# Striped expert channels, VectorE transposes and a split x in the expert stage of a two-layer streaming encoder on one core

## The chip, the core and the metric

The kernel runs on one core of one Trainium2 chip. The metric is the device time of one execution in microseconds (us). Before the change its median over 3 runs is 1421.37 us (1417.27 to 1430.04). All data is float32; "f32r" below is the rounded float32 type; a product of two f32r operands is one instruction of TensorE in the trace, a plain float32 product two.

## What is computed

Two layers over 256 tokens of width 1024. Each has a modulated norm, a convolution branch and an attention branch, an output product and a residual; then a feed-forward part. Layer 0 has a dense one. Layer 1 has eight experts, of which each token uses the two with the largest router logits:

```python
def moe_swiglu(h, w_router, b_router, w_gate, w_up, w_down):
    t = h.reshape(B * S, D)                                   # 256 x 1024
    logits = (t @ w_router) + b_router
    top_val, top_idx = lax.top_k(logits, TOP_K)               # TOP_K = 2
    top_w = jax.nn.softmax(top_val, axis=-1)
    combine = sum(one_hot(top_idx, 8) * top_w[..., None], axis=1)
    for e in range(8):                                        # w_gate, w_up: 1024 x 3584, w_down: 3584 x 1024
        out = out + combine[:, e:e + 1] * ((silu(t @ w_gate[e]) * (t @ w_up[e])) @ w_down[e])
```

The weights of the eight experts are 352 MB, three quarters of what the kernel reads.

## The kernel before, in words

Layer 0 and the attention half of layer 1 are untouched by the change, except for a small constant built at the start. All that follows is `moe`, the expert stage.

Tokens are dispatched. The experts are put into eight slots: slot 0 is expert 0, slots 1 to 7 hold the others by falling token count. `CAPS` gives each slot's room in groups of 32 tokens: (3, 4, 3, 3, 3, 2, 2, 2). Slot 1 with four groups is called wide, the rest narrow. `dispatch(e, pm)` makes the slot's tokens: `pick` compares token positions with a ramp and gives a 0/1 matrix `pm` (token x place), `gather` multiplies x by it on TensorE and applies the modulation, and a second product turns `pm` around into `pT`, which `combine` later uses to add the results back to their tokens. For a narrow slot `pT` comes from 8 products per group with the identity (L1076), for the wide one from two transposes (L1055).

An expert's 3584 hidden channels are walked in 7 pieces of 512. A unit is one slot and one piece: `gu_mm` (gate and up products, `silu`, product), `h_T` (transpose of the hidden piece on TensorE, copied back by ScalarE) and `dn_mm` (down product, accumulated in PSUM). Narrow slots use the four column strips of the TensorE array: in `streams` (L1089) a stationary block of 128 x 32 (one k block of one token group) is loaded into strip j, and 256 weight columns move past it; four strips work on four quarters of the columns side by side. The wide slot uses 128 x 128 stationary blocks and three f32r products of split operands (`mm3`, L254 to L256); ScalarE makes the high part of each weight tile (L140), VectorE the low part (L148).

TensorE's order is written out by hand. In each step of the unit loop: gate/up of unit n, then the down product of unit n-1, then the transposes of unit n, then, where due, a dispatch. `units` interleaves two lanes of slots, `LANES`; lane 1 starts three units (`STAGGER`) after lane 0. So with (0, 2, 1, 3) and (5, 4, 6, 7) the slot pairs that run together are 0/5, 2/5, 2/4, 1/4, 1/6, 3/6, 3/7.

Weights arrive in tiles of 1 MB (128 x 2048), all issued by SyncE (SP) in the order of use, six tiles per unit. The ring of buffers has 15 tiles where only narrow slots are near (9 `raw`, 3 `hi`, 3 `lo`), and 9 near the wide slot, whose high and low parts need the other six; a few spare buffers help at the start. A tile is loaded again when the last product that reads it is done. x stays in `x_sb`; the result gathers in a separate tile, `macc`.

Of the kernel before, what the change touches and what calls it, by code (L numbers as in the profile page):

```python
# [9 lines left out]
F32 = mybir.dt.float32  # L10
# [7 lines left out]
P = 128  # L18
D = 1024
# [18 lines left out]
LANES = (0, 2, 1, 3), (5, 4, 6, 7)  # L38
STAGGER = 3
NR = NE - 1  # L40
# [13 lines left out]
def kernel(ctx, tc, x, cvec, wada, bada, wga, wqkv, wout, wfgu, wfd, wfd2,  # L54
# [44 lines left out]
    for l in range(2):  # L99
        for n, w in (("ng1", 8), ("ng2", 8), ("cw", 4 * CW), ("cb", 4), ("lg", 4), ("lb", 4), ("qg", 1), ("kg", 1)):  # L100
# [14 lines left out]
                   allow_small_or_imprecise_dtypes=True)  # L115
    cs = const.tile([P, KT], F32, name="cs")
# [790 lines left out]
    def moe(acc, g_bc, mm, A, B, AW, bw):  # L907
        y = [None, None]
        oh = const.tile([P, 2, NT, NE], F32, name="oh")
# [106 lines left out]

        def gather(pm, n, put):

            for q in range(2):
                ps = bank("ps_g").rearrange("p (j s) -> p j s", j=4)  # L1020
                f = a2("xf", [P, 4, P])
                for j in range(4):
                    k = 4 * q + j
                    for t in range(NT):
                        nc.tensor.matmul(ps[:, j, 0:n], x_sb[:, t, k * P:(k + 1) * P], pm[:, 1, t, 0:n],  # L1025
                                         start=t == 0, stop=t == NT - 1)
                for j in range(4):
# [3 lines left out]
                put(slice(4 * q, 4 * q + 4), f[:, :, 0:n])  # L1031

        def dispatch(e, pm):


            g, n = CAPS[e], 32 * CAPS[e]
            src = gates if e else comb
            if wide(e):
                xg = a8("xg", [P, 2, KT, P], F32R)

                def put(js, f):
                    nc.scalar.activation(xg[:, 0, js, :], f, AF.Copy)
                    nc.vector.tensor_tensor(xg[:, 1, js, :], f, xg[:, 0, js, :].bitcast(F32), op=ALU.subtract)
            else:
                xg = a8("xn", [P, KT, n])

                def put(js, f):
                    nc.vector.tensor_copy(xg[:, js, :], f)

            gather(pm, n, put)  # L1050
            ps = bank("ps_ws")
            ws = sm.tile([P, 4], F32, tag="ws", name="ws")
            if wide(e):
                for tt in range(NT):
                    nc.tensor.transpose(ps[:, tt * P:(tt + 1) * P], pm[:, 0, tt, :], ident)  # L1055
                for tt in range(NT):
                    nc.tensor.matmul(ps[:, S:S + 1], pm[:, 0, tt, :], src[:, tt, e:e + 1], start=tt == 0,
                                     stop=tt == NT - 1)
                pT = a4("pmT", [P, S], F32R)
                nc.scalar.activation(pT, ps[:, 0:S], AF.Copy)  # L1060
                nc.vector.tensor_copy(ws[:, 0:1], ps[:, S:S + 1])
                return xg, pT, ws
            for t in range(g):
                for tt in range(NT):
                    for j in range(4):
                        nc.tensor.matmul(ps[32 * j:32 * j + 32, t:t + 1], pm[:, 0, tt, 32 * t:32 * t + 32],
                                         src[:, tt, e:e + 1], start=tt == 0, stop=tt == NT - 1)
            nc.vector.tensor_copy(ws[:, 0:g], ps[:, 0:g])
            pT = a4("pmT", [P, g, S], F32R)
            for b in range(0, g, 2):  # L1070
                ps = bank("ps_w").rearrange("p (t s) -> p t s", t=2)
                m = min(2, g - b)
                for t in range(m):
# [18 lines left out]
        def gu_mm(e, between):  # L1092


            g, xg = CAPS[e], disp[e][0]
# [10 lines left out]
            else:  # L1106
                pv = [p_.rearrange("p (t u s) -> p t u s", t=2, u=2) for p_ in ps]
# [19 lines left out]
        def h_T(hm, g, split=False):  # L1127
# [46 lines left out]
        def combine(e, ys, out_=None):  # L1174
# [12 lines left out]
            for b in range(0, 4, 2):  # L1187
# [10 lines left out]
                for i in range(2):  # L1198
                    sl = slice(256 * (b + i), 256 * (b + i) + 256)
                    nc.vector.tensor_tensor(macc[:, :, sl], (macc if e else x_sb)[:, :, sl], pss[i], op=ALU.add)  # L1200
# [7 lines left out]
        def rest(e):  # L1208

            pm = pick(lambda t: posm[:, t, 0:1])  # L1210
            xg = a8("xr", [P, KT, P])
            gather(pm, P, lambda js, f: nc.scalar.activation(xg[:, js, :], f, AF.Copy))
            ps = bank("ps_w")
            for t in range(NT):
                nc.tensor.transpose(ps[:, t * P:(t + 1) * P], pm[:, 0, t, :], ident)
            for t in range(NT):
                nc.tensor.matmul(ps[:, 2 * P:2 * P + 1], pm[:, 0, t, :], comb[:, t, 0:1], start=t == 0,
                                 stop=t == NT - 1)
# [67 lines left out]
        shares()  # L1286
        disp, accs = {0: dispatch(0, pm)}, {}
# [5 lines left out]
        with tc.manual_schedule():  # L1293
# [6 lines left out]
            for n, (e, c) in enumerate(units):  # L1300
# [15 lines left out]
                hm = gu_mm(e, between)  # L1316
                if n == 1:
# [11 lines left out]
                for pe, ys in early:  # L1329
                    if pe == 0:  # L1330
                        macc = a8("macc", [P, NT, D])
                    combine(pe, ys)
# [8 lines left out]
                pend = e, c, h_T(hm, CAPS[e], wide(e))  # L1341
# [170 lines left out]
```

## Time and profile before

| what | value |
|---|---|
| median of 3 runs | 1421.37 us (1417.27 to 1430.04) |
| the profiled execution: its time | 1421.24 us |
| its span (first to last instruction) | 1419.2 us |
| mean granted TensorE clock | 0.987 of 2.4 GHz |
| TensorE (PE) busy | 1349.9 us, 95% of the span |
| weight loads into the array (PEld) | 973.1 us, 69% |
| VectorE (DVE) / ScalarE (ACT) | 565.3 us, 40% / 398.4 us, 28% |
| read from HBM | 470.01 MB, 332 GB/s over the span |

The expert stage runs from 513 us, where the first slot is gathered, to the end. A row of a view of groups reads: line, engine, operation, output <- inputs, shapes, count | busy us, mean ns of one | idle time just before it and what ended most of it. Instructions of TensorE overlap, so count times mean is more than busy; the pace is read from the start of a run of instructions to the start of the next.

### The profile page before, as it was taken

Reading aid. Unit: us, or ns where it says so; the run is one execution under the profiler, and the core shown is the slowest. Engines: PE = TensorE matmul, PEld = TensorE weight load, DVE = VectorE, ACT = ScalarE, POOL = GpSimd, SP = SyncE. Lnnn points to the kernel's source line nnn. Section 1 sums busy time; section 2 is a strip of 40 time slices with the busy share of each in tenths; the row PEclk is TensorE's granted clock in tenths of the full one; section 3 lists DMA queues with packets and bytes.
Section 4 is the critical chain, followed back from the end, with each engine's and each line's share of the span. In section 5 each row is a group of like instructions: output and inputs, shape, how many; then the busy total and the mean of one; then the engine's idle time right before and its main releaser. Section 6 shows DMA issues by size and latency. Waiting matters only on the chain.

```text
span 1419.2 us, 38942 instructions
## 1 busy us (share of the span) xinstructions
PE 1349.9 (95%) x17604; PEld 973.1 (69%) x17604; DVE 565.3 (40%) x1025; ACT 398.4 (28%) x635; POOL 3.0 (0%) x17
## 2 busy tenths in 40 slices
PE   4998899999899999999999999999999999999886
PEld 4877699999697686657666656677667766665453
DVE  3597677777689651000100100354455430010011
ACT  3335444433456330101001001334333420100000
POOL 0000000000000000000000000000000000000000
PEclk9999999999999999999999999999999999999998
DMA  9963787878551579899999995989898999999995
GB/s 383 418 243 123 263 308 273 305 272 307 172 205 45 206 292 369 342 417 417 417 417 417 417 417 223 396 350 362 327 379 346 397 417 417 417 417 417 417 418 202
DMA packets 66379, 473.64 MB, mean 334 GB/s; under 512 B 7840, under 2 KB 7968, under 8 KB 9248
## 3 DMA queue, kind: packets, MB, share of 16 engines
q1 hardware_dynamic: 66208, 471.09, 83.3%
q8 instruction: 140, 2.29, 0.6%
q14 instruction: 31, 0.25, 0.0%
HBM read 470.01 MB, written 1.05 MB: 332 GB/s over the span
## 4 chain that ended last, share of the span: by engine, by line
PE 77%; DMA 13%; DVE 5%; ACT 3%; issue 1%; SPq 0%; DVEq 0%; ACTq 0%
PE ps_gu L1089 23%; PE ps_d L1089 13%; DMA raw<-in_wmgu 6%; DMA raw<-in_wmd 6%; PE ps_ga L256 4%; PE ps_ga L254 4%; PE ps_ga L255 4%; PE ps_g L1025 2%; PE ps_y L708 2%; PE ps_gu L256 2%; PE ps_gu L254 2%; PE ps_gu L255 2%; DVE cv L544 2%; PE ps_ada L308 1%; DVE lo L148 1%; PE ps_hT L1130 1%
## 5 line engine op out<-in xcount | busy, mean ns | idle before, releaser
L1089 PE MATMUL ps_gu<-raw,xn 128*32 128x256 f32 x8064 | 450.2, 380 | 4.1 <-DMA raw<-in_wmgu 3.9
L1089 PEld LDWEIGHTS ps_gu<-raw,xn 128*32 128x32 f32 x8064 | 269.1, 110 | 169.2 <-DMA raw<-in_wmgu 7.8
L148 DVE TENSOR_TENSOR lo<-raw,hi 128x2048 fp32r<-128x2048 f32 x99 | 225.5, 2289 | 84.7 <-ACT hi L140 82.0
L1123 DVE TENSOR_TENSOR mh<-ps_gu,sg 128x256 f32<-128x256 f32 (+1 forms) x91 | 32.7, 382 | 547.2 <-ACT sg L1120 547.2
L1089 PE MATMUL ps_d<-raw,hT 128*32 128x256 f32 x4032 | 232.3, 381 | 8.0 <-DMA raw<-in_wmd 7.5
L140 ACT ACTIVATE hi<-raw 128x2048 fp32r<-128x2048 f32 x99 | 188.3, 1912 | 107.2 <-PE ps_ga L256 43.0
L1089 PEld LDWEIGHTS ps_d<-raw,hT 128*32 128x32 f32 x4032 | 133.7, 110 | 96.6 <-DMA raw<-in_wmd 9.9
L1120 ACT ACTIVATE sg<-ps_gu 128x256 f32<-128x256 f32 (+1 forms) x91 | 32.0, 352 | 426.3 <-PE ps_gu L1089 380.7
L254 PE MATMUL ps_ga<-hThi,lo 128*128 128x256 f32 x480 | 137.5, 287 | 7.6 <-ACT hThi L446 7.6
L256 PE MATMUL ps_ga<-hTlo,hi 128*128 128x256 f32 x480 | 136.9, 285 | 0.8 <-DVE hTlo L451 0.8
L255 PE MATMUL ps_ga<-hThi,hi 128*128 128x256 f32 x480 | 136.3, 284 | 0.0
L254 PEld LDWEIGHTS ps_ga<-hThi,lo 128*128 128x128 f32 x480 | 92.9, 194 | 8.7 <-ACT hThi L446 8.4
L256 PEld LDWEIGHTS ps_ga<-hTlo,hi 128*128 128x128 f32 x480 | 92.4, 192 | 1.4 <-DVE hTlo L451 1.4
L255 PEld LDWEIGHTS ps_ga<-hThi,hi 128*128 128x128 f32 x480 | 92.4, 193 | 0.2
L544 DVE SCALAR_TENSOR_TENSOR cv<-zp,cols_sb,cv 128x256 f32<-128x256 f32 x206 | 85.4, 477 | 0.0
L1137 ACT ACTIVATE hT<-ps_hT 128x384 f32<-128x384 f32 (+1 forms) x49 | 21.8, 445 | 221.4 <-PE ps_hT L1130 221.4
L347 DVE SCALAR_TENSOR_TENSOR ada_acc<-raw,cs,ada_acc 128x512 f32<-128x512 f32 x63 | 47.2, 749 | 1.2
L256 PE MATMUL ps_gu<-lo,xg 128*128 128x512 f32 x112 | 44.3, 396 | 1.3 <-DVE lo L148 1.3
L254 PE MATMUL ps_gu<-hi,xg 128*128 128x512 f32 x112 | 44.8, 400 | 0.0
L255 PE MATMUL ps_gu<-hi,xg 128*128 128x512 f32 x112 | 44.3, 396 | 0.0
L308 PE MATMUL ps_ada<-raw,crep 128*32 128x128 f32 x960 | 34.4, 302 | 7.4 <-DMA raw<-in_wada 7.1
L308 PEld LDWEIGHTS ps_ada<-raw,crep 128*32 128x32 f32 x960 | 29.2, 121 | 11.2 <-issue 8.3
(263 smaller groups left out, 1310.1 us busy)
## 6 DMA issues: line engine op xcount, KB each, us to landing
raw<-in_wmgu SPq DMA_DIRECT2D x222, 1024.0 KB, 13.9
raw<-in_wmd SPq DMA_DIRECT2D x111, 1024.0 KB, 14.3
raw<-in_wada SPq DMA_DIRECT2D x48, 1024.0 KB, 6.2
raw<-in_wfgu SPq DMA_DIRECT2D x22, 1024.0 KB, 6.0
raw<-in_wqkv SPq DMA_DIRECT2D x12, 1024.0 KB, 6.6
raw<-in_wfd SPq DMA_DIRECT2D x11, 1024.0 KB, 6.5
raw<-in_wga SPq DMA_DIRECT2D x8, 1024.0 KB, 10.6
raw<-in_wout SPq DMA_DIRECT2D x8, 1024.0 KB, 7.7
```

The costliest lines, as they stand in the source:

```text
L140: nc.scalar.activation(hi[:, i * w:(i + 1) * w], r, AF.Copy)
L148: nc.vector.tensor_tensor(lo[:, w], r, hi[:, w].bitcast(F32), op=ALU.subtract)
L254: nc.tensor.matmul(o_, a[1], b[0], start=first, stop=False)
L255: nc.tensor.matmul(o_, a[0], b[0], start=False, stop=False)
L256: nc.tensor.matmul(o_, a[0], b[1], start=False, stop=last)
L308: nc.tensor.matmul(ps[32 * g:32 * g + 32, 0:P], crep[:, j, :], w(j)[:, g * P:(g + 1) * P], start=j == 0, stop=j == KT - 1)
L347: nc.vector.scalar_tensor_tensor(accs[ch], ws[ch](j), cs[:, j:j + 1], accs[ch], op0=ALU.mult, op1=ALU.add)
L544: nc.vector.scalar_tensor_tensor(cv[:, a, :], zp[:, a, i:i + S], cw[:, a, i:i + 1], cv[:, a, :], op0=ALU.mult, op1=ALU.add)
L708: nc.tensor.matmul(acc[t][hf], yf[:, k, t * P:(t + 1) * P], w(k // 2, 2 * (k % 2) + hf), start=k == 0, stop=False)
L1089: nc.tensor.matmul(ps[t // 2][32 * j:32 * j + 32, t % 2], x(t), w(j), start=first and t % 2 == 0, stop=last, skip_group_check=True)
L1120: nc.scalar.activation(sg[:, 2 * b:2 * b + m, :], v[:, 0:m, 0, :], AF.Silu)
L1123: nc.vector.tensor_tensor(hm[:, 2 * b:2 * b + m, :], v[:, 0:m, 1, :], sg[:, 2 * b:2 * b + m, :], op=ALU.mult)
```

## The change

1. `gu_mm` of a narrow slot. A weight tile pair m (256 gate and 256 up columns) is now multiplied by itself: for each k block one stationary block per strip and 128 moving columns, taken as 4 runs of 32 columns with a step of 128. Each strip thus holds, for every token, hidden channels striped so that a 32 x 32 block transpose gives the layout that the down product wants.
2. The hidden piece is turned by one VectorE `transpose` (32 x 32 blocks), `h_T` of a narrow slot does nothing, and TensorE's transposes and ScalarE's copy of them go. The wide slot keeps them.
3. x times its norm factor is split once, after unit 2, into f32r high and low parts (`split_x`); every `gather` but slot 0's multiplies both by the f32r `pm`.
4. `pT`: `row` spreads the positions of the 256 tokens over all partitions by two products with the identity, and VectorE compares them with the constant `spot`.
5. `macc` is `x_sb` itself; its old place holds other tiles (`home` for the gathered tokens of six slots).
6. The lanes become (0, 1, 2, 3) and (5, 6, 4, 7). Pairs: 0/5, 1/5, 1/6, 2/6, 2/4, 3/4, 3/7. The two halves of a gate/up tile pair are also loaded in the new order of use.

```diff
-LANES = (0, 2, 1, 3), (5, 4, 6, 7)
+LANES = (0, 1, 2, 3), (5, 6, 4, 7)
...
-        plan += [(of_slot(wmgu, e, *p), 4096 if wide(e) else 0) for p in (parts if wide(e) else zip(*parts))]
+        plan += [(of_slot(wmgu, e, *p), 4096 if wide(e) else 0) for p in parts]
...
-            pm = a2("pm", [P, 2, NT, P])
+            pm = a2("pm", [P, NT, P], F32R)
             for t in range(NT):
-                nc.vector.tensor_scalar(pm[:, 1, t, 0:n], iota_f[:, 0:n], col(t), y[t], op0=ALU.is_equal,
-                                        op1=ALU.mult)
-            for t in range(NT):
-                nc.vector.tensor_scalar(pm[:, 0, t, 0:n], iota_f[:, 0:n], col(t), None, op0=ALU.is_equal)
+                nc.vector.tensor_scalar(pm[:, t, 0:n], iota_f[:, 0:n], col(t), None, op0=ALU.is_equal)
...
+        def split_x():
+            hi = a8("xh", [P, NT, D], F32R)
+            lo = a8("xl", [P, NT, D], F32R)
+            for t in range(NT):
+                nc.scalar.activation(hi[:, t], x_sb[:, t], AF.Copy, scale=y[t])
+            for t in range(NT):
+                nc.vector.scalar_tensor_tensor(lo[:, t], x_sb[:, t], y[t], hi[:, t].bitcast(F32), op0=ALU.mult,
+                                               op1=ALU.subtract)
...
+                ops = [(v, pm[:, t, 0:n]) for t in range(NT) for v in parts[0][t]]
...
-                    for t in range(NT):
-                        nc.tensor.matmul(ps[:, j, 0:n], x_sb[:, t, k * P:(k + 1) * P], pm[:, 1, t, 0:n],
-                                         start=t == 0, stop=t == NT - 1)
+                    for i, (v, m) in enumerate(ops):
+                        nc.tensor.matmul(ps[:, j, 0:n], v[:, k * P:(k + 1) * P], m, start=i == 0,
+                                         stop=i == len(ops) - 1)
...
+        def row(col):
+            ps = bank("ps_w")
+            for t in range(NT):
+                nc.tensor.matmul(ps[:, t * P:(t + 1) * P], col(t).to_broadcast([P, P]), ident, start=True, stop=True)
+            return ps[:, 0:S]
...
-                        for j in range(4):
-                            nc.tensor.matmul(ps[32 * j:32 * j + 32, t, tt * P:(tt + 1) * P],
-                                             pm[:, 0, tt, 32 * (b + t):32 * (b + t) + 32], ident, start=True, stop=True)
-                nc.scalar.activation(pT[:, b:b + m, :], ps[:, 0:m, :], AF.Copy)
+                for t in range(g):
+                    nc.vector.tensor_scalar(pT[:, t, :], r, spot[:, 4 + t:5 + t], None, op0=ALU.is_equal)
...
-                for h in range(2):
+                pv = [p_.rearrange("p (t m a s) -> p t m a s", t=2, m=2, a=4) for p_ in ps]
+                for m in range(2):
                     w = whole(3)
-                    for i in range(4):
-                        k = 4 * h + i
-                        wk_ = [w(a, i).rearrange("p (u j s) -> p u j s", u=2, j=2) for a in range(2)]
-                        streams(pv, g, lambda t: xg[:, k, 32 * t:32 * t + 32], lambda j: wk_[j // 2][:, :, j % 2],
-                                k == 0, k == KT - 1)
+                    for k in range(KT):
+                        wk_ = w(k // 4, k % 4).rearrange("p (a j s) -> p j a s", a=4, j=4)
+                        streams([v[:, :, m] for v in pv], g, lambda t: xg[:, k, 32 * t:32 * t + 32],
+                                lambda j: wk_[:, j], m == 0 and k == 0, k == KT - 1)
...
+                hT = a2("hT", [P, g, P])
+                nc.vector.transpose(hT.rearrange("p t s -> p (t s)"), hm.rearrange("p t s -> p (t s)"))
+                return hT
...
-        def h_T(hm, g, split=False):
+        def h_T(hm, g, split=False, narrow=False):
+            if narrow:
+                return hm
...
                 hm = gu_mm(e, between)
+                if n == STAGGER - 1:
+                    parts.append(split_x())
```

How the instructions move is shown at three places. First TensorE before, at the end of slot 5's third unit, where slot 2 is dispatched: `ps_gu` is gate/up, `ps_d` the down product, `ps_hT` the transposes, `ps_g`, `ps_ws` and `ps_w` the dispatch.

```order
L1089 MATMUL ps_d_6035<-raw,hT 32x256 x32
L1130 MATMUL ps_hT<-ident,mh 128x128 x3
L1025 MATMUL ps_g<-pm,x_sb 128x96 x16
L1066 MATMUL ps_ws<-rt,pm 32x1 x24
L1076 MATMUL ps_w<-ident,pm 32x128 x24
L1089 MATMUL ps_gu_6458<-raw,xn 32x256 x64
L1089 MATMUL ps_d_5319<-raw,hT 32x256 x8
```

There the transposes follow the down product, then the dispatch, then the next unit.

TensorE after the change, the dispatch of slot 5 after unit 2 and the gate/up of the next unit (lines are those of the changed kernel):

```order
L1048 MATMUL ps_g<-pm,xh 128x64
L1048 MATMUL ps_g<-pm,xl 128x64
L1093 MATMUL ps_ws<-rt,pm 32x1 x16
L1060 MATMUL ps_w<-ident,rt 128x128 x2
L1114 MATMUL ps_gu_5886<-raw,xn 32x128 x8
L1114 MATMUL ps_gu_5887<-raw,xn 32x128 x4
```

The transposes between the down product and the next unit are gone, `ps_w` is 2 products in place of 24 (16 for a slot of two groups), the gather alternates the two parts of x, and a gate/up product has 128 moving columns, not 256.

TensorE after the change where the wide slot begins: slot 0's last unit, slot 5's unit, then slot 1.

```order
L1114 MATMUL ps_d_6553<-raw,hT 32x256 x32
L1114 MATMUL ps_gu_7534<-raw,xn 32x128 x128
L1114 MATMUL ps_d_5494<-raw,hT 32x256 x8
L1114 MATMUL ps_d_5495<-raw,hT 32x256 x4
L261 MATMUL ps_gu_7745<-hi,xg 128x512
L262 MATMUL ps_gu_7745<-hi,xg 128x512
L263 MATMUL ps_gu_7745<-lo,xg 128x512
```

A two-group unit has 128 gate/up products where it had 64, and the wide slot now follows slot 0; before, slot 2 stood there.

VectorE after the change, around unit 2: `mh` is the hidden piece, `xl` the low part of x, `xn` the gathered tokens.

```order
L1151 TENSOR_TENSOR mh<-ps_gu_5547,sg 128x256
L1151 TENSOR_TENSOR mh<-ps_gu_5548,sg 128x128
L1154 STREAM_TRANSPOSE hT<-mh 128x384
L1029 SCALAR_TENSOR_TENSOR xl<-x_sb,ny,xh 128x1024 x2
L1080 COPY xn<-xf 128x256 x2
L1095 COPY ws<-ps_ws 128x2
L1103 TENSOR_SCALAR pmT<-ps_w,spot 128x256 x2
```

The block transpose stands right behind the product that it turns, the split of x behind that, and the comparisons that make `pT` come last, where ScalarE copied a product before.

## Rows read from the trace of the kernel before

**Rows 1.** Busy time of each engine, five stretches of the expert stage.
```profile
core 0: us, PE busy (x) PEld busy (x) DVE busy (x) ACT busy (x) POOL busy (x), PEclk, DMA share, GB/s
519.00:860.00 341.00, 339.10 (x6097) 219.83 (x6097) 34.02 (x108) 38.07 (x97) 0.00 (x0) 1.00 0.99 404
860.00:920.00 60.00, 58.66 (x926) 37.11 (x926) 14.67 (x18) 15.81 (x25) 0.00 (x0) 1.00 0.74 290
920.00:1150.00 230.00, 228.54 (x2515) 163.59 (x2517) 111.31 (x97) 93.48 (x96) 0.00 (x0) 0.99 0.91 365
1150.00:1285.00 135.00, 135.00 (x2393) 82.86 (x2385) 14.03 (x33) 13.53 (x34) 0.00 (x0) 1.00 1.01 417
1285.00:1400.00 115.00, 103.44 (x1736) 58.18 (x1732) 8.54 (x18) 7.38 (x18) 0.00 (x0) 0.99 0.99 408
```

**Rows 2.** Costliest groups of the page: narrow products, and layer modulation in the 128-column form.
```profile
L1089 PE MATMUL ps_gu<-raw,xn 128*32 128x256 f32 x8064 | 450.2, 380 | 4.1 <-DMA raw<-in_wmgu 3.9
L1089 PE MATMUL ps_d<-raw,hT 128*32 128x256 f32 x4032 | 232.3, 381 | 8.0 <-DMA raw<-in_wmd 7.5
L308 PE MATMUL ps_ada<-raw,crep 128*32 128x128 f32 x960 | 34.4, 302 | 7.4 <-DMA raw<-in_wada 7.1
```

**Rows 3.** What SP's DMA queue waited for, 480 to 1420 us: total, times, longest.
```profile
SPq L131 <- PE ps_gu L1089: 248.4, 62, 9.6
SPq L131 <- PE ps_d L1089: 144.9, 34, 10.8
```

**Rows 4.** Chain of work in order of time (start, us, what): pairs 0/5 and 2/4.
```profile
660.32 10.50 PE ps_gu L1089 x192
...
674.27 0.48 PE ps_hT L1130 x3
...
686.98 0.37 PE ps_hT L1130 x2
687.35 10.50 PE ps_gu L1089 x192
...
809.18 10.50 PE ps_gu L1089 x192
...
841.50 10.50 PE ps_gu L1089 x192
```

**Rows 5.** The same chain: pairs 1/4 and 1/6, from one narrow down product to the next.
```profile
925.76 5.32 PE ps_d L1089 x96
...
959.50 5.32 PE ps_d L1089 x96
...
1069.91 3.59 PE ps_d L1089 x64
...
1098.36 3.59 PE ps_d L1089 x64
```

**Rows 6.** Timeline of PE: a burst of 128-column products, and one gate/up run of 256 columns.
```profile
504.68 1.96 PE L308 MATMUL ps_ada<-raw,crep 128*32 128x128 f32 x64
...
600.85 10.57 PE L1089 MATMUL ps_gu<-raw,xn 128*32 128x256 f32 x192
```

**Rows 7.** The chain again: dispatches of a two-group and a three-group slot.
```profile
571.39 0.92 PE ps_w L1076 x32
...
642.37 3.55 PE ps_g L1025 x32
...
646.41 1.36 PE ps_w L1076 x48
```

**Rows 8.** The chain at the first unit's end, and one f32r product of 512 columns.
```profile
529.70 0.39 ACT sg L1120
...
530.12 0.44 DVE mh L1123
...
1056.63 0.23 PE ps_d L255
```

**Rows 9.** Groups by form, 440 to 1420 us: transposes, and a VectorE copy.
```profile
L1130 PE MATMUL ps_hT<-ident,mh 128*128 128x128 f32 x154 | 28.7, 290 | 0.5 <-DVE mh L1123 0.5
...
L1048 DVE COPY xn<-xf 128x384 f32<-128x384 f32 x8 | 2.9, 360 | 23.1 <-ACT xf L1029 23.1
```

More of the change, by code (lines that the diff above doesn't have):

```diff
@@ L37 @@
 CAPS = (3, 4, 3, 3, 3, 2, 2, 2)
-LANES = (0, 2, 1, 3), (5, 4, 6, 7)
+LANES = (0, 1, 2, 3), (5, 6, 4, 7)
 STAGGER = 3
+HOME = (0, None, 0, None, 768, 768, 1536, 1536)
 NR = NE - 1
@@ L115 @@
                    allow_small_or_imprecise_dtypes=True)
+    spot = const.tile([P, 8], F32, name="spot")
+    nc.gpsimd.iota(spot[:, 0:4], pattern=[[32, 4]], base=1, channel_multiplier=1, allow_small_or_imprecise_dtypes=True)
+    for v in range(4):
+        nc.vector.tensor_scalar(spot[32 * v:32 * v + 32, 4:8], spot[32 * v:32 * v + 32, 0:4], -32.0 * v, None,
+                                op0=ALU.add)
     cs = const.tile([P, KT], F32, name="cs")
@@ L908, in moe @@
         y = [None, None]
+        macc, parts = x_sb, []
         oh = const.tile([P, 2, NT, NE], F32, name="oh")
@@ L1015, in slot_pick @@
             return pick(lambda t: src[:, t, e:e + 1], 32 * CAPS[e])
-        def gather(pm, n, put):
+        def split_x():
[6 more added lines that the diff above has]
+                                               op1=ALU.subtract)
+            return [(hi[:, t], lo[:, t]) for t in range(NT)]
+        def gather(pm, n, put):
+            if not parts:
+                sm_ = a2("pmy", [P, NT, P])
+                for t in range(NT):
+                    nc.vector.tensor_scalar(sm_[:, t, 0:n], pm[:, t, 0:n].bitcast(F32), y[t], None, op0=ALU.mult)
+                ops = [(x_sb[:, t], sm_[:, t, 0:n]) for t in range(NT)]
+            else:
+                ops = [(v, pm[:, t, 0:n]) for t in range(NT) for v in parts[0][t]]
             for q in range(2):
@@ L1031, in gather @@
                 put(slice(4 * q, 4 * q + 4), f[:, :, 0:n])
+        def row(col):
+            ps = bank("ps_w")
+            for t in range(NT):
+                nc.tensor.matmul(ps[:, t * P:(t + 1) * P], col(t).to_broadcast([P, P]), ident, start=True, stop=True)
+            return ps[:, 0:S]
         def dispatch(e, pm):
             g, n = CAPS[e], 32 * CAPS[e]
-            src = gates if e else comb
+            src, at = (gates, places) if e else (comb, posm)
+            pf = pm.bitcast(F32)
             if wide(e):
@@ L1044, in dispatch @@
             else:
-                xg = a8("xn", [P, KT, n])
+                xg = a8("xn", [P, G]) if HOME[e] is None else home[:, HOME[e]:HOME[e] + KT * n]
+                xg = xg[:, 0:KT * n].rearrange("p (k n) -> p k n", k=KT)
                 def put(js, f):
@@ L1054, in dispatch @@
                 for tt in range(NT):
[L1055 to L1061, printed above, removed]
@@ L1062, in dispatch @@
-                return xg, pT, ws
-            for t in range(g):
-                for tt in range(NT):
-                    for j in range(4):
[L1066 to L1073, printed above, removed]
+                    nc.tensor.matmul(ps[:, 0:1], pf[:, tt, :], src[:, tt, e:e + 1], start=tt == 0, stop=tt == NT - 1)
@@ L1079, in dispatch @@
+            r = row(lambda t: at[:, t, e:e + 1])
+            if wide(e):
+                pT = a4("pmT", [P, S], F32R)
+                nc.vector.tensor_scalar(pT, r, spot[:, 0:1], None, op0=ALU.is_equal)
+            else:
+                pT = a4("pmT", [P, g, S], F32R)
+                for t in range(g):
+                    nc.vector.tensor_scalar(pT[:, t, :], r, spot[:, 4 + t:5 + t], None, op0=ALU.is_equal)
             return xg, pT, ws
@@ L1199, in combine @@
                     sl = slice(256 * (b + i), 256 * (b + i) + 256)
-                    nc.vector.tensor_tensor(macc[:, :, sl], (macc if e else x_sb)[:, :, sl], pss[i], op=ALU.add)
+                    nc.vector.tensor_tensor(macc[:, :, sl], macc[:, :, sl], pss[i], op=ALU.add)
                 if out_:
@@ L1210, in rest @@
             pm = pick(lambda t: posm[:, t, 0:1])
+            pf = pm.bitcast(F32)
             xg = a8("xr", [P, KT, P])
@@ L1214, in rest @@
             for t in range(NT):
-                nc.tensor.transpose(ps[:, t * P:(t + 1) * P], pm[:, 0, t, :], ident)
+                nc.tensor.transpose(ps[:, t * P:(t + 1) * P], pf[:, t, :], ident)
             for t in range(NT):
-                nc.tensor.matmul(ps[:, 2 * P:2 * P + 1], pm[:, 0, t, :], comb[:, t, 0:1], start=t == 0,
+                nc.tensor.matmul(ps[:, 2 * P:2 * P + 1], pf[:, t, :], comb[:, t, 0:1], start=t == 0,
                                  stop=t == NT - 1)
@@ L1286, in moe @@
         shares()
+        home = a8("xn", [P, G])
         disp, accs = {0: dispatch(0, pm)}, {}
@@ L1340, in moe @@
                     ahead(2)
-                pend = e, c, h_T(hm, CAPS[e], wide(e))
+                pend = e, c, h_T(hm, CAPS[e], wide(e), not wide(e))
                 if nxt is not None:
```

21 lines of the change are left out of this document (18 added, 3 removed).

## The prediction

> **What bounds the kernel now.** First I read the busy time by stretches of the expert stage [rows 1]. From 519 to 1285 us TensorE is busy in 761 of 766 us, the granted clock at 0.99 to 1.00: it sets the pace there. From 1285 to 1400 us it is busy in 103.4 of 115, and the DMA share is 0.99: there the weights set the pace and TensorE waits 11.6 us, in the down and gate/up products, for `in_wmd` (7.5 us) and `in_wmgu` (3.9 us) [rows 2]. So the stage has two limits close together. A weight tile of 1.049 MB at 417 GB/s takes 2.51 us, six of them 15.1 us, a pair of units 30.2 us. TensorE, read from one gate/up to the same place a pair later, takes 27.0 us for the pair 0/5 and 32.3 for 2/4 [rows 4], 33.7 for 1/4 and 28.4 for 1/6 [rows 5]. Summed over the stretches, TensorE works 865 us and the tiles moved (342 MB) need 821 us. The DMA stood idle for some 58 us before 1150 us (rates of 404, 290 and 365 against 417 GB/s [rows 1]) because SP waited for TensorE to release buffers, 248 us behind gate/up and 145 us behind the down products [rows 3], and it lacked that time at the end, where light pairs (27.0 us of TensorE against 30.2 of DMA) emptied the ring.
>
> So a microsecond taken from TensorE before 1285 us counts fully: it also lets SP go on sooner. At the end it counts only if the ring no longer runs dry.
>
> **Part by part.** The sum is made against the profiled execution, 1421.24 us (span 1419.2 and 2.0 around it), which is the median of the runs shown within 0.2 us.
>
> *Transposes of narrow slots.* They stand on TensorE between the down product and the next gate/up: 0.48 us for three groups and 0.37 for two [rows 4]. Slots 0, 2, 3, 4 have 28 units of three groups, slots 5, 6, 7 have 21 of two: 28 x 0.48 + 21 x 0.37 = 21.2 us, the 126 of the 154 transposes that are not the wide slot's [rows 9]. In the first unit there is no down product between, so TensorE also waits 0.39 + 0.44 us for ScalarE and VectorE [rows 8]; that 0.8 us goes too, since the next gate/up now follows at once. Sum: -22.0 us.
>
> *The VectorE transpose in their place.* The trace has none. Its nearest row is the copy of 128x384 at 0.36 us [rows 9]; from below it is bounded by nothing, from above I take four such copies, 1.4 us. It is hidden in either case: its result is wanted after a whole further gate/up, over 7 us for two groups (128 instructions at 53 ns), and silu, product and transpose need 0.39 + 0.44 + 1.4 us after the end of their own. I take 0. If VectorE fell so far behind in the wide stretch (busy 111 of 230 us [rows 1]) that this cover were gone, at most 1.4 us would stand in a unit. The Trainium skill, "VectorE: DVE Perf Modes", section "The three transpose paths", gives 311 ns for 128x128 bf16 in 32x32 blocks on VectorE, which would make an estimated 0.9 us here; no row shows it, and it would be hidden as well.
>
> *Gate/up in 128 columns.* 8064 instructions of 256 columns become 16,128 of 128. The pace of 256 is (10.57 - 0.38) / 191 = 53.4 ns, the run of 192 less its last instruction [rows 6, 2]. For 128 columns with 128x32 blocks there are bursts: 64 instructions in 1.96 us, less 0.30 for the last, give 26.4 ns [rows 6, 2]; 48 against 32 instructions of `ps_w` differ by 0.44 us, 27.5 ns each [rows 7]. So 430.6 us become 425.8 to 443.5, that is -5 to +13; I take the middle, 26.95 ns, +4 us. The columns now come in runs of 32. Before, gate/up read two runs of 128 and the down product one of 256, and their durations are 380 and 381 ns [rows 2], so one jump costs nothing; three jumps have no row. The upper bound is the mean of the whole 128-column group, 34.4 us / 960 = 35.8 ns [rows 2], which would be +147 us; it holds starts and tails of short bursts, so I take the bursts themselves. It is the first rival below.
>
> *Turning `pm` around.* `ps_w` cost 1.36 us for three groups and 0.92 for two [rows 7]; now it is 2 products with 128x128 blocks, 4 instructions. At the gather's pace of 3.55 / 32 = 0.11 us [rows 7] that is 0.44. Four slots save 0.92, three save 0.48, the wide one trades 2 instructions for 4 (+0.2): -4.9 us. The comparisons on VectorE are wanted only when the slot is finished, seven units later: 0.
>
> *Gather from the split x.* Before: 16 float32 products of two instructions each; now 32 f32r products of one. 32 instructions with a 128x128 block and 64 to 128 columns before and after, and 3.55 us for 96 columns is 0.11 us each, more than 96 columns at the pace of [rows 6] need, so the block's load sets it. I take 0. Bounds for seven slots: at 26.4 ns each -19 us; at 0.23 us, what an f32r product of 512 columns takes [rows 8], +27 us. The split itself (two ScalarE and two VectorE instructions of 1024 columns, some 1 us each by the copy's 0.36 for 384) comes after unit 2's gate/up, beside a down product of 5.3 us [rows 5], and ends some 4 us into it: hidden, and at most 4 us, once, if not. Slot 0's gather now waits for one more pair of VectorE instructions: +0.4 us.
>
> *x in place of `macc`, `home`, the constant at the start.* Nothing of these is on TensorE; the store at the end is the same. 0.
>
> *The order of the lanes.* Before, after the last heavy pair came 4 of 1/6, 3 of 3/6, 4 of 3/7 and 3 units of slot 7 alone: against the DMA -1.8, -3.2, -3.2 each and some -4 for a unit alone (192 instructions at 53.4 ns and 0.37 us against 15.1), -41 us in all, against one or two dispatches of some 5 us, four combines, and a ring of 9 tiles (22.6 us) at the end of the wide slot. It ran dry at 1285 us. Now 2/4 and 3/4 come late: 32.3 less two transposes is 31.4, +1.2 each, so in those seven pairs the ring of 15 tiles (38 us) fills; after them come only 4 of 3/7 and 3 units alone, some -29 us, with one dispatch and three or four combines against it. The light pairs 0/5 and 1/5, 1/6 stand at the start, where the ring is full and five dispatches help. So the 11.6 us at the end go: -11.6. What is late next is the DMA itself: 821 us of tiles against 865 - 23 = 842 us of TensorE, 21 us of margin.
>
> Sum: -22.0 + 4 - 4.9 + 0.4 - 11.6 = -34.1 us: **1387.1 us**, 2.4% faster.
>
> **Rivals.** *The pace of 128 columns does not hold (slower).* Place: gate/up of all narrow units. The rows at 27 ns are bursts of 48 and 64; now runs of 256 and 384 follow each other, with twice the weight loads and moving runs of 32 columns. For: PEld is already busy 0.64 of the stretch from 519 us [rows 1], and the group mean is 35.8 ns. Against: the bursts show no slowing. Above 26.95 + 34.1 us / 16,128 = 29.1 ns the change loses. Half way between 27.5 and 35.8, at 31.6 ns, it costs 75 us: 1462 us. The Trainium skill's "TensorEngine Tiling (Array Packing)", section "Instruction Overhead", speaks against the change in the same place: some 60 cycles of overhead for each product. By that rule, 25 ns for 8064 more instructions shared by four strips, the estimate is 50 us and a time of 1437 us. The trace so far disagrees: 26.4 against 53.4 ns leaves no room for it.
>
> *The ring still runs dry at the end.* If the DMA, not TensorE, ends the stage, what TensorE gains after 1285 us turns into waiting. Its gains before that, some 36 of 49 narrow units, are 0.73 x 22.5 = 16 us, and SP follows them: about 1404 us. For it: the margin of 21 us is less than the 58 us for which the DMA stood, and the wide slot still has only 9 tiles. Against it: the pairs above.
>
> *The f32r gather is slow below 256 columns.* No row has one. At 0.23 us an instruction, +27 us: 1414 us. Against: 64 to 128 columns should not take what 512 take.
>
> *Nothing changes because the weights bound everything.* Excluded but for 3%: the tiles need 821 us, TensorE 865.
>
> **Chances.** Forecast 0.66, dry ring 0.12, slow gather 0.08, pace 0.11, others 0.03. The range goes from 1368 (gate/up at its low end, -9, and half of the gather's low bound, -10) to 1408 (past the dry ring, without the slow gather at its full price and the pace); about 0.18 lies outside. A measurement can tell about 1% from no change, 14 us: below 1407 lie the forecast, the dry ring and most of a milder slow gather, 0.84; within 1% 0.06; slower 0.10.
>
> **What would show it.** Right: no transposes of narrow slots on TensorE, gate/up of three groups in 10.3 to 10.6 us for 384 instructions, `ps_g` at 3.5 us, `ps_w` at 0.44, hardly any wait for `in_wmd` and `in_wmgu` in the last 115 us, a DMA share under 1 there. Wrong: gate/up runs over 11.2 us (29.1 ns), an idle TensorE ahead of `ps_d` put down to the VectorE transpose, waits for weights at the end, or gathers over 5 us.

## The result: a tenth slower

The changed kernel takes 1567.12 us (median of 4 runs, 1558.43 to 1569.90), the kernel before 1420.53 us in the same comparison: a ratio of 1.1015, 95% interval 1.0955 to 1.1075, or +146 us. The forecast was 1387.1 us. The profiled execution took 1565.86 us, with a span of 1564.2 us.

The page of the changed kernel, its two narrow products (columns as for [rows 2]):

```profile
L1114 PE MATMUL ps_gu<-raw,xn 128*32 128x128 f32 x16128 | 492.6, 280 | 110.9 <-issue 108.8
L1114 PE MATMUL ps_d<-raw,hT 128*32 128x256 f32 x4032 | 242.8, 387 | 14.4 <-issue 12.2
```

Where gate/up waited 4.1 us in all, and for weights [rows 2], it now stands idle 110.9 us, and 108.8 of that is put down to "issue": nothing that the profile shows was missing, no operand, no buffer, no other engine. The busy time is 42 us higher as well. Stretches of the expert stage (columns as for [rows 1]):

```profile
519.00:860.00 341.00, 301.03 (x6495) 256.56 (x6496) 101.83 (x153) 76.93 (x101) 0.00 (x0) 0.97 0.85 333
...
1000.00:1290.00 290.00, 243.02 (x6834) 215.07 (x6827) 29.47 (x71) 14.45 (x44) 0.00 (x0) 0.98 0.85 326
1290.00:1560.00 270.00, 230.86 (x6186) 205.74 (x6185) 31.16 (x68) 12.22 (x34) 0.00 (x0) 0.94 0.80 306
```

In [rows 1] either TensorE or the DMA was full in every stretch. Here TensorE is busy 0.84 to 0.88 of the time, the DMA share is 0.80 to 0.85: neither sets the pace. The timeline shows what the idle time looks like (start, length, run of like instructions, in brackets the idle time ahead of it):

```profile
635.10 3.70 PE L1114 MATMUL ps_gu<-raw,xn 128*32 128x128 f32 x128 [2.50 <-issue]
...
649.49 3.70 PE L1114 MATMUL ps_gu<-raw,xn 128*32 128x128 f32 x128 [0.68 <-issue]
655.42 1.18 PE L1114 MATMUL ps_gu<-raw,xn 128*32 128x128 f32 x34 [2.22 <-issue]
...
672.30 3.70 PE L1114 MATMUL ps_gu<-raw,xn 128*32 128x128 f32 x128 [2.51 <-issue]
```

A product is counted here and below as the trace counts it, one instruction of TensorE. Between a pause and the next stand 128 products or a multiple of it, but for a few records that the trace lacks (98 + 3 + 1 + 61 + 92 = 255 between 639.92 and 649.49 us). Their pace is what the prediction took: (3.70 - 0.28) / 127 = 26.9 ns. So the array is not slow; it is left without instructions. The page's list of DMA queues has a queue that loads instructions (packets, MB, share), in the kernel before and in the changed one:

```profile
q8 instruction: 140, 2.29, 0.6%
```

```profile
q8 instruction: 200, 3.28, 0.8%
```

TensorE has 25,284 products instead of 17,604, each with its weight load. 60 packets more for 7,680 such pairs more: 128 pairs a packet of 16.4 KB, the length of the runs between pauses.

**Theory T1:** TensorE's instructions come in blocks of 128 pairs. While weights stream in, a block needs longer to come than 128 products of 128 columns need to run; with 256 columns (128 x 53.4 ns = 6.8 us) it was hidden. T1a says the weights' transfers delay the blocks, T1b that each block has a fixed latency. **Rivals:** T2, the array or its weight load is slower for 128 columns in long runs (the prediction's first rival); T3, moving columns in four pieces of 32 are slow; T4, another part of the change costs.

### The profile page after: what moved, and what is told of

Same layout as the page of the kernel before. It is cut to its first block, busy times and chain, and to the rows that moved or that the text cites. A ratio compares the mean times of both kernels' runs of the same rounds, so it can differ in the third digit from the quotient of the medians.

```text
span 1564.2 us, 54245 instructions
## 1 busy us (share of the span) xinstructions
PE 1377.7 (88%) x25284; PEld 1184.5 (76%) x25284; DVE 597.5 (38%) x1085; ACT 370.9 (24%) x576; POOL 3.1 (0%) x18
## 4 chain that ended last, share of the span: by engine, by line
PE 82%; issue 9%; DVE 5%; ACT 3%; DMA 1%; SPq 0%; DVEq 0%; ACTq 0%
PE ps_gu L1114 30%; PE ps_d L1114 14%; PE ps_ga L263 3%; PE ps_ga L261 3%; PE ps_ga L262 3%; PE ps_g L1048 2%; PE ps_y L715 2%; PE ps_gu L263 2%; PE ps_gu L262 2%; PE ps_gu L261 2%; PE ps_ada L315 1%; DVE cv L551 1%; PE ps_f L262 1%; PE ps_f L261 1%; PE ps_f L263 1%
## 5 line engine op out<-in xcount | busy, mean ns | idle before, releaser
L1114 PE MATMUL ps_gu<-raw,xn 128*32 128x128 f32 x16128 | 492.6, 280 | 110.9 <-issue 108.8
L1114 PEld LDWEIGHTS ps_gu<-raw,xn 128*32 128x32 f32 x16128 | 464.6, 113 | 133.5 <-issue 127.1
L1151 DVE TENSOR_TENSOR mh<-ps_gu,sg 128x256 f32<-128x256 f32 (+1 forms) x77 | 26.5, 372 | 640.1 <-ACT sg L1148 640.1
L1114 PE MATMUL ps_d<-raw,hT 128*32 128x256 f32 x4032 | 242.8, 387 | 14.4 <-issue 12.2
L1114 PEld LDWEIGHTS ps_d<-raw,hT 128*32 128x32 f32 x4032 | 164.0, 112 | 79.1 <-issue 27.3
L1148 ACT ACTIVATE sg<-ps_gu 128x256 f32<-128x256 f32 (+1 forms) x77 | 23.9, 343 | 704.2 <-PE ps_gu L1114 678.6
L261 PE MATMUL ps_f<-hi,hl 128*128 128x512 f32 x88 | 35.5, 404 | 0.0
```

Of the source, the lines that this page charges most:

```text
L261: nc.tensor.matmul(o_, a[1], b[0], start=first, stop=False)
L1114: nc.tensor.matmul(ps[t // 2][32 * j:32 * j + 32, t % 2], x(t), w(j), start=first and t % 2 == 0, stop=last, skip_group_check=True)
L1151: nc.vector.tensor_tensor(hv[0][:, 2 * b:2 * b + n], v[:, 0:n, :, 64:128], sv[0][:, 2 * b:2 * b + n], op=ALU.mult)
```

## Experiments

**1. Only the split, in the kernel before.** Same mathematics, contiguous columns, twice the products:

```diff
-streams(pv, g, lambda t: xg[:, k, 32 * t:32 * t + 32], lambda j: wk_[j // 2][:, :, j % 2],
-        k == 0, k == KT - 1)
+for u in range(2):
+    streams([v[:, :, u] for v in pv], g, lambda t: xg[:, k, 32 * t:32 * t + 32],
+            lambda j: wk_[j // 2][:, u, j % 2], k == 0 and u == 0, k == KT - 1)
```

> The kernel before, with only gate/up's product of 256 columns issued as two products of 128 contiguous columns on the same weight tile: 16,128 products instead of 8,064, nothing else changed. T1 (TensorE's instructions come too slowly: they arrive in blocks of 128 products with their weight loads, a block of 128-column products is done in about 3.5 us and the next one is not there yet): slow like the changed kernel, 1540 to 1610 us, with runs of 128 products and pauses of 2 to 2.5 us 'issue' between them. T2 (the array itself, or its weight load, has a lower pace for 128 columns when the run is long): the same time, but the products stand evenly at 31 ns or more, without pauses. T3 (the moving operand of four pieces of 32 columns is what is slow): 1415 to 1430 us, no change. T4 (another part of the change, the gather in two parts or VectorE's transposes, is what costs): 1415 to 1430 us.

Measured: 1627.1 us, ratio 1.1437 (1.1412 to 1.1462), +204 us. The timeline:

```profile
912.96 3.70 PE L1089 MATMUL ps_gu<-raw,xn 128*32 128x128 f32 x128 [1.65 <-issue]
919.72 0.95 PE L1089 MATMUL ps_gu<-raw,xn 128*32 128x128 f32 x25 [3.06 <-issue]
```

The slowdown, the 128 and the pauses (154.0 us of "issue" ahead of the two narrow products) come with the count of products alone. T3 and T4 are out as its cause; T2 finds no slower pace. The time is above the 1610 that T1 allowed: the pauses are 33 us more than the changed kernel's 121.0, and this kernel keeps the old order of experts and the transposes.

**2. The change at 256 columns.** A weight tile of gate/up is laid out on the host as 4 rows of channels by all 512 + 512 columns of a piece (before: 8 rows by 256 + 256), so that each strip takes 8 runs of 32 columns; wide slot and overflow code follow.

```diff
-gu = np.empty((NE, N_GU, P, KT, 2, 256), ...)
+gu = np.empty((NE, N_DN, 2, P, 4, 2, 512), ...)
...
-    w = whole(3)
-    for k in range(KT):
-        wk_ = w(k // 4, k % 4).rearrange("p (a j s) -> p j a s", a=4, j=4)
-        streams([v[:, :, m] for v in pv], ...)
+    w = whole(3, 2)
+    for i in range(4):
+        k = 4 * m + i
+        wk_ = w(i // 2, i % 2).rearrange("p (r j s) -> p j r s", r=8, j=4)
+        streams(pv, ...)
```

> The changed kernel with all its parts, but a weight tile of gate/up holds 4 rows of input channels by all 512 gate and 512 up channels of a chunk instead of 8 rows by half of them, so a stripe is 256 columns again: 8,064 products of 8 pieces of 32 columns. T1: the pauses of 'issue' go; the sum of the prediction without its gate/up term is left, 1421 - 38 = 1383 us, 1370 to 1400. T2: the same, 1370 to 1400. T3 (pieces of 32 columns are slow): 1500 us or more, since the pieces stay. T4: 1520 to 1570 us, since every other part stays.

Measured: 1388.4 us, ratio 0.9742 (0.9709 to 0.9776): no pause left, and a kernel that beats both. From the page:

```profile
L1114 PE MATMUL ps_gu<-raw,xn 128*32 128x256 f32 x8064 | 450.0, 383 | 0.3 <-DVE rt L985 0.2
L1114 PE MATMUL ps_d<-raw,hT 128*32 128x256 f32 x4032 | 227.4, 379 | 1.2 <-DMA raw<-in_wmd 1.2
```

Eight pieces of 32 columns don't slow the products (T3), and the other parts of the change together gain (T4). Between the ratios of this run and of the change lie 0.127, 181 us: the price of 128 columns.

**3 and 4. Both kernels without the weights' traffic.** In `need`, every chunk after the first three is one that already lies on chip; those loads are left out, so the output is not the reference's.

```diff
 i = len(raws)
 ap, n = plan[i]
+if i > first_gu + 2:
+    raws.append(raws[first_gu + 1 + i % 2])
+    continue
```

> The changed kernel in which the experts' weights after the first three chunks are not loaded: every later chunk computes on one of two that lie on chip already, so those loads are left out and the output is another. TensorE's instructions are the same. T1a (the blocks of instructions come late because they share the DMA engines with the weights): the pauses of 'issue' in the experts' part fall from about 110 us to under 20 us, and the time to 1380 to 1450 us. T1b (a block has a fixed latency whatever the weights do): the pauses stay at 90 us or more, 1530 to 1570 us. T2: no pauses, but products at 31 ns or more, 1530 to 1570 us.

> The kernel before with the same edit: the experts' weights after the first three chunks are not loaded, and later chunks compute on two that lie on chip. It is the base for the run of the changed kernel without these loads. Its waits for weights go, so 1330 to 1400 us under every theory, with hardly a pause of 'issue'. T1a: the changed kernel without loads comes within 40 us of it. T1b and T2: the changed kernel without loads is 100 us or more slower than it.

Measured: 1394.33 us (changed, 128 columns) and 1403.48 us (before), one run each. The changed kernel without this traffic:

```profile
L1117 PE MATMUL ps_gu<-raw,xn 128*32 128x128 f32 x16128 | 454.0, 274 | 0.8 <-DVE rt L988 0.6
```

The same 16,128 products from as many blocks (199 packets), and no pause at all: the pauses need the traffic, T1a. T1b and T2 fall. (Run 4 lies 3 us above its range.) What 128 columns cost where no weights stream is read against run 4, which has 256:

```profile
L1092 PE MATMUL ps_gu<-raw,xn 128*32 128x256 f32 x8064 | 445.3, 380 | 0.0
```

That is +8.7 us, at a mean granted clock of 0.979 in run 3 against 0.987 in run 4; the prediction had +4, and -5 to +13 as its bounds.

The trace also has the start and the end of each packet of the instruction queue. Every pause of "issue" from 520 us on, 77 in the changed kernel and 93 in run 1, ends 1.2 to 1.6 us after such a packet has landed, and so do those of runs 5 and 6. So it is the packet that TensorE waits for. A packet takes no longer beside the weights than without them (0.98 us on average in the changed kernel from 520 us on, 1.06 in run 3): it starts late.

**5. Half of the traffic.** As run 3, but only every second chunk is left out (`i % 2`, the chunk before is used again); the output is not the reference's.

> The changed kernel in which every second chunk of the experts' weights (after the first three) is not loaded and the chunk before it is used again, so half of the loads are left out and the output is another. T1a (the blocks of instructions share the DMA engines with the weights): the pauses of 'issue' lie between those with all weights (123 us) and with none (0), 5 to 70 us, and the time between 1394 and 1567 us, 1400 to 1500. If only a full queue delays the blocks, the pauses are near 0; if every transfer beside them does, near 60 us.

Measured: 1481.65 us, 67.6 us of pauses from 520 us on, in the view of waits:

```profile
PE ps_gu L1117 <- issue: 58.5, 39, 2.9
PE ps_d L1117 <- issue: 9.1, 8, 1.6
```

That is about half of the 121 us at full traffic, on these two products, and without traffic there are none. But the sum doesn't tell a full queue from any transfer beside a block, as the expectation wanted it to, because the loads that are left come in bursts. Stretches of this run (columns as for [rows 1]; the granted clock is 1.00 in all):

```profile
1320.00:1330.00 10.00, 10.00 (x310) 9.62 (x305) 4.06 (x8) 1.23 (x2) 0.00 (x0) 1.00 0.02 5
1330.00:1340.00 10.00, 10.00 (x280) 7.99 (x276) 1.30 (x3) 0.00 (x0) 0.00 (x0) 1.00 0.02 3
1340.00:1350.00 10.00, 10.00 (x312) 8.63 (x308) 1.20 (x3) 0.55 (x2) 0.00 (x0) 1.00 0.01 3
1350.00:1360.00 10.00, 8.34 (x266) 7.28 (x262) 0.87 (x2) 0.38 (x1) 0.00 (x0) 1.00 0.99 392
```

TensorE is full where the DMA engines stand still and pauses where they are full. In the 2 us before the awaited packet starts, the DMA share is 0.87 or more at each of the 47 pauses; of all 167 packets in that part of the run, only 69 start behind a share over 0.9. So the pauses of this run stand behind full or nearly full DMA engines; whether a lighter load would delay a block too isn't shown.

**6. Half of the splits.** Only odd k are split; 12,096 products.

```diff
+if k % 2 == 0:
+    streams(...)
+    continue
 for u in range(2):
```

> The kernel before with gate/up's product of 256 columns split into two of 128 for every second row of input channels only: 12,096 products, 32 KB blocks as before. A block of 128 products then lasts about 4.6 us (two thirds at 27 ns, one third at 54 ns), against 3.45 in the run with all split and 6.9 in the kernel before. T1: the pauses become shorter (about 6.0 - 4.6 = 1.4 us instead of 2.5) and fewer; 1440 to 1540 us, that is less than half of the 204 us that all splits cost, since supply and use meet between 4.6 and 6.9 us. If the cost goes by the count of products alone (T2, a price for each), it is half: 1515 to 1535 us, without pauses.

(The blocks have 16.4 KB; the 32 KB there is a slip.) Measured: 1485.4 us, ratio 1.0439 (1.0385 to 1.0494), +63 us, under a third of the 204. The timeline:

```profile
648.27 4.98 PE L1089 MATMUL ps_gu<-raw,xn 128*32 128x128 f32 x128 [1.76 <-issue]
654.19 1.08 PE L1089 MATMUL ps_gu<-raw,xn 128*32 128x128 f32 x32 [0.94 <-issue]
```

A block lasts 4.98 us and the pause is 0.94: 5.92 us from block to block. In run 1 it is 6.76 at the place shown. In the changed kernel two pauses follow each other with one block between them 39 times, at 4.0 to 6.8 us; half of these distances lie between 5.7 and 6.2 (649.49 to 655.42: 5.93). The pause fills up what the block's own work leaves of about 6 us. It isn't a price for each product (T2).

**7. The new order alone.**

```diff
-LANES = (0, 2, 1, 3), (5, 4, 6, 7)
+LANES = (0, 1, 2, 3), (5, 6, 4, 7)
```

> The kernel before with the new order of the experts alone, (0, 1, 2, 3) and (5, 6, 4, 7) instead of (0, 2, 1, 3) and (5, 4, 6, 7): the expert that the transfers carry at full precision is worked earlier, the rest is as before. The prediction gave the order 11.6 us, because the last 115 us then wait less for weights: 1405 to 1415 us, and TensorE's waits for weights after 1290 us, 25 us before, fall under 12 us. The rival that the weights still run dry at the end: 1417 to 1427 us, the waits as before.

Measured: 1399.01 us, ratio 0.9848 (0.9812 to 0.9884), -22 us. The page:

```profile
L1089 PE MATMUL ps_gu<-raw,xn 128*32 128x256 f32 x8064 | 445.5, 380 | 0.0
L1089 PE MATMUL ps_d<-raw,hT 128*32 128x256 f32 x4032 | 227.0, 379 | 0.5 <-ACT hT L1137 0.5
```

That is below the 1405 to 1415 us expected. Against [rows 2], the 11.4 us of waits for weights are gone, and the busy time falls by 10.0 us besides (450.2 to 445.5, 232.3 to 227.0). Run 4, in the old order but with no weights to wait for, has nearly the same 445.3 and 226.9. So some 10 us that come with late weights had been counted as busy, and the term was twice what the view of waits showed. How much of them is waits too short to be listed, and how much the ends of the products before a wait, was not taken apart.

**8. Order and stripes of 256 with VectorE's transposes, in the kernel before.**

```diff
+hT = a2("hT", [P, g, P])
+nc.vector.transpose(hT.rearrange("p t s -> p (t s)"), hm.rearrange("p t s -> p (t s)"))
```

(with the layout and order of runs 2 and 7; gather and scatter matrices as before)

> The kernel before with two parts of the change: the new order of the experts, and striped channels with VectorE's transposes, at 256 columns a stripe; the gather with the scaled matrix, and the scatter matrices by TensorE, stay as before. It takes TensorE's transposes (21 us by the prediction) from the run with the order alone (1399 us). If the gain of the stripes is what the prediction says, 1399 - 21 = 1378 us, 1372 to 1384, and it is then 10 us faster than the changed kernel at 256 columns, whose new gather and scatter matrices cost granted clock (0.66 to 0.83 for 10 us behind its dispatches, 0.71 and 0.78 at its first one). If the dips come from VectorE's transposes or from the stripes, the dips stay and the time is that of the changed kernel at 256 columns, 1385 to 1392 us.

Measured: 1387.32 us, ratio 0.9775 (0.9744 to 0.9806): 10 us under run 7, not 21. Its chain of waits at the end:

```profile
1311.37 6.91 PE ps_gu L1089 x128
1318.28 5.18 PE ps_d L1089 x96
1323.46 1.50 PE ps_gu L1089 x27
1324.96 21.02 DMA raw<-in_wmd
1346.10 20.19 DMA raw<-in_wmd
1366.33 3.67 PE ps_d L1089 x60
```

No transposes stand between the products any more, but from 1325 to 1366 us, of a span of 1383.3, the chain hangs on weights. TensorE waits 6.9 us for them after 1280 us, where run 7 has no such wait, and its narrow products are 5.3 us busier than there (677.8 against 672.5 us). TensorE has caught up with the DMA: the rest of the gain has turned into this. The time is that of the expectation's other branch, but not for its reason: in stretches of 10 us from 510 to 1370 us the granted clock is 1.0 but for 0.95 and 0.88 at 790 to 810 us, and run 7, without these parts, has 0.83 at 800.

**9. The changed kernel at 256 columns, first expert mended.** The scaled matrix of slot 0 is made straight from the positions, ahead of `pm`, in place of from `pm`.

```diff
+if e == 0:
+    ...
+    nc.vector.tensor_scalar(sm_[:, t, 0:32 * CAPS[0]], iota_f[:, 0:32 * CAPS[0]], src[:, t, 0:1], y[t],
+                            op0=ALU.is_equal, op1=ALU.mult)
```

> The changed kernel at 256 columns, with the scaled selection matrix of the first expert made straight from the positions ahead of the plain one, as the kernel before does, instead of from the plain one behind other work of VectorE. In the changed kernel TensorE waits 2.6 us for it and the granted clock is 0.71 and 0.78 in the 20 us behind (5 us of work). If that wait is the cause: the wait falls under 1 us, the clock stays at 1.0 there, and the time falls by 5 to 8 us, to 1380 to 1384 us. If the dip has another cause: 1386 to 1391 us and the dip stays.

Measured: 1379.98 us, ratio 0.9720 (0.9688 to 0.9751). TensorE's wait for that matrix (view of waits) and the 20 us around it (stretches, columns as for [rows 1]), first in run 2:

```profile
PE ps_g L1048 <- DVE pmy L1038: 2.6, 1, 2.6
```

```profile
510.00:520.00 10.00, 7.19 (x100) 6.60 (x97) 6.24 (x34) 2.64 (x5) 0.00 (x0) 0.71 0.65 218
520.00:530.00 10.00, 9.67 (x125) 8.42 (x129) 2.93 (x12) 4.08 (x9) 0.00 (x0) 0.78 1.01 420
```

and then in this run:

```profile
PE ps_g L1052 <- DVE pmy L1023: 0.5, 1, 0.5
```

```profile
510.00:520.00 10.00, 9.18 (x155) 7.52 (x151) 6.30 (x31) 5.85 (x12) 0.00 (x0) 1.00 0.96 363
520.00:530.00 10.00, 10.00 (x192) 7.32 (x188) 4.44 (x24) 0.67 (x2) 0.00 (x0) 1.00 1.01 423
```

The long wait is gone and so is the dip. But the wait didn't start the dip. In shorter stretches of run 2, the clock falls to 0.50 (1.2 GHz) while TensorE is still busy, before its wait of 2.6 us begins at 517.1 us:

```profile
512.00:514.00 2.00, 2.00 (x40) 1.98 (x44) 1.64 (x9) 0.00 (x0) 0.00 (x0) 1.00 0.04 8
514.00:516.00 2.00, 2.00 (x47) 1.62 (x36) 1.11 (x7) 0.00 (x0) 0.00 (x0) 0.55 0.69 172
516.00:518.00 2.00, 1.14 (x9) 1.04 (x5) 0.75 (x5) 1.76 (x3) 0.00 (x0) 0.50 1.03 340
```

And run 10, whose wait there is 0.5 us, dips as well, for a shorter time:

```profile
510.00:512.00 2.00, 2.00 (x29) 1.91 (x32) 1.64 (x10) 0.00 (x0) 0.00 (x0) 0.66 0.03 8
512.00:514.00 2.00, 2.00 (x44) 1.85 (x40) 0.77 (x5) 0.00 (x0) 0.00 (x0) 0.50 0.86 201
```

What starts the dip stays open; the wait may make it longer. The median falls by 8 us, by the two ratios 3 us, and the two intervals overlap as do the runs (1374.73 to 1386.92 here, 1382.8 to 1395.7 in run 2): what the edit is worth in time is not settled.

**10. Run 8 with the scatter matrices on VectorE.** `row` and the comparisons with `spot` as in the change; only the gather is as before.

```diff
-    nc.tensor.matmul(ps[32 * j:32 * j + 32, t, tt * P:(tt + 1) * P],
-                     pm[:, 0, tt, 32 * (b + t):32 * (b + t) + 32], ident, start=True, stop=True)
+r = row(lambda t: (places if e else posm)[:, t, e:e + 1])
+...
+    nc.vector.tensor_scalar(pT[:, t, :], r, spot[:, 4 + t:5 + t], None, op0=ALU.is_equal)
```

> The run of the kernel before with the new order and stripes of 256, and the scatter matrices made on VectorE from a broadcast row of positions (4 products in place of 48) as well; only the gather stays as before. The prediction gave these matrices 4.9 us: 2 to 6 us faster than the run without them, 1372 to 1378 us, with the clock at 1.0 behind the dispatches, if the dips of the changed kernel come from the gather in two parts. If the 4 products of the row, or the wait in front of them, bring the dips: not faster than the run without them, and 0.66 to 0.83 behind the dispatches.

Measured: 1378.27 us, ratio 0.9703 (0.9675 to 0.9731), 10 us under run 8. It has the lowest ratio of all, level with run 9 within the intervals. That is more than the 2 to 6 us expected, and the products themselves don't account for it: TensorE's busy time in `ps_w` falls by 3.6 us, from 9.3 to 5.7. The waits for weights fall from 6.9 to 2.5 us and the narrow products are 5.8 us less busy (672.0 against 677.8), although TensorE has less to do; why, stays open. The granted clock doesn't decide between the two branches: in stretches of 10 us it is 0.83 at 510, 540 and 800 us, and run 7 has the last of these too.

## Why the prediction was wrong

**Gate/up in 128 columns: predicted +4 us, measured about +181 (run 2 against the change).** This is the step that failed, in the sentence "it holds starts and tails of short bursts, so I take the bursts themselves". The pace was right: 26.9 ns inside a run, and +8.7 us in all, inside the bounds of -5 to +13, where no weights stream (run 3 against run 4). But the bursts that gave the pace [rows 6] had 64 products, half a block: they could not show what happens when one block ends and the next must be there. At 256 columns and 53.4 ns a product a block is used up in 6.8 us, just above the 6 us that one takes to come; halving the columns halved the 6.8 and crossed that line. The bill of the changed kernel against run 2, from the profiled executions: 121.0 us of "issue" ahead of the two products, and 58.0 us more of busy time in them ((492.6 + 242.8) - (450.0 + 227.4)), together 179, against 170.2 between the spans. Of the 58, an estimate gives about 20 to the tails of the 75 runs that end in a pause (0.28 us of the last product, otherwise covered by the next), 4 to 9 to the pace and some 7 to the granted clock (mean 0.964 against 0.973 over the span); the rest, more than 20 us, was not taken apart.

**The first rival had the place, the sign and the point from which it decides, and the wrong mechanism.** It priced a lower pace at 1462 us. Its break-even of 29.1 ns holds: gate/up takes (492.6 + 110.9) / 16,128 = 37.4 ns a product, idle time included. In the runs of products shown none was slow. The prediction's sentence on the Trainium skill's "TensorEngine Tiling (Array Packing)", section "Instruction Overhead", put 50 us on the same place; the runs show no such price (454.0 against 445.3 us in runs 3 and 4). The rule that bore on it was another: the Trainium skill, "Runtime: NRT & Kernel Launch", section "Instruction fetch mechanics", says that instructions come in blocks of 16 KiB, 256 instructions, over a DMA queue of their own, and that crossing a block is mostly hidden. The runs agree with the block (16.4 KB, 128 pairs) and disagree with "mostly hidden" as soon as a block is used up in 3.4 us beside streaming weights.

**The sum of everything else was -38.1 us and run 2 measured -37 (0.9742 of 1421), but not by its parts: that the two agree is luck.** The order of the experts gave -22 instead of -11.6: the view of waits holds only what shows as idle, and nearly as much again lay in the busy time of the products (run 7). Transposes and first-unit wait gave -10 instead of -22.0: TensorE's 21 us were saved, and half was lost again to weights at the end (run 8). That is the second rival, the dry ring, in part; the margin of 21 us of DMA was too thin. The scatter matrices gave -10 instead of -4.9 (run 10), of which 3.6 is their own time on TensorE. The gather with slot 0's wait may have cost some 5 us instead of 0.4 (run 2 against run 10), but the intervals overlap.

**Slot 0's gather: +0.4 us predicted.** The second pair of VectorE instructions stands behind other work on its queue, so TensorE waits 2.6 us, and the clock, down since before the wait (run 9), stays down while the gather runs: in run 2 it takes 6.04 us for 32 products, in run 7 3.83 us. The seven later gathers take 3.49 to 4.04 us in the changed kernel's chain, 3.74 on average, against 3.54 before. One of them, with `ps_w`:

```profile
798.86 3.49 PE ps_g L1048 x32
...
802.71 0.64 PE ps_w L1060 x4
```

The bound of that rival was 0.23 us a product, 7.4 us a gather, so the third rival (a slow f32r gather) did not occur; `ps_w` takes 0.64 where 0.44 was forecast.

**VectorE's transposes: hidden, as said.** From the view by form of the changed kernel:

```profile
L1154 DVE STREAM_TRANSPOSE hT<-mh 128x384 f32<-128x384 f32 x28 | 16.2, 578 | 1.0
L1154 DVE STREAM_TRANSPOSE hT<-mh 128x256 f32<-128x256 f32 x21 | 9.4, 446 | 0.7
```

On average they take 0.58 and 0.45 us, under the 1.4 taken as the bound, and no product waited for them. The estimate of 0.9 us from the Trainium skill, "VectorE: DVE Perf Modes", section "The three transpose paths", was too high as well.

## What to carry to other kernels

Where the count of TensorE's instructions is to rise, divide a block's worth of them by their time: here a block of 128 product and weight-load pairs came every 6 us beside streaming weights, so by an estimate (6.0 us / 128) products of less than some 47 ns each starve TensorE, with idle time put down to "issue" and runs of 128 between the pauses. A pace read from bursts shorter than a block says nothing of long runs. And of a stripe, keep the columns and change the layout in memory: the same idea at 256 columns is 2.6% faster than the kernel before, where at 128 it was 10% slower.

## What was not expected of the hardware

- Instructions come late beside data: 0, 68 and 121 us of pauses with none, half and all of the experts' weights loaded, from a queue that itself takes 0.8% of the DMA engines' time. The packets start late rather than move slowly; what holds them back was not tried.
- Moving columns in 8 pieces of 32 run as fast as in 2 pieces of 128: 444.5 us for 8,064 products in run 10, 445.5 in run 7.
- Late weights also show as busy time: 10.0 us beside the 11.4 that the view of waits named (runs 4 and 7).
